# A hybrid mLSTM and DeltaNet block on one core: the turned tiles' transfers go from ScalarE to SyncE, a transpose is put off, and the bodies of four engines are ordered anew

## The chip, the cores and the metric

The kernel runs on one core of a Trainium2 chip. The metric is the device time of one execution in microseconds; the time of a kernel is the median of several executions. The profile shows one execution.

## The reference

The input x has 512 tokens of 2048 channels. The block computes, in float32:

```
u   = rmsnorm(x) * norm_w
p   = u @ w_in                          # 512 x 20528, split into the parts below
mLSTM branch:     q, k, v, o-gate, z-gate, i, f    # 8 heads, 128 wide q and k, 256 wide v
DeltaNet branch:  q, k, v, z-gate, beta, decay     # 16 heads of 128
merge gates:      g1, g2                           # 2048 each
h1 = rmsnorm_head(mlstm(q, k, v, i, f)) * w * sigmoid(o) * silu(z)
h2 = rmsnorm_head(deltanet(conv_silu(q), conv_silu(k), conv_silu(v), beta, decay)) * w * silu(z)
y  = x + sigmoid(g1) * (h1 @ w_out[0:2048]) + sigmoid(g2) * (h2 @ w_out[2048:4096])
out = rmsnorm(y) * final_norm_w
```

DeltaNet normalises q and k per token, and solves per chunk a unit lower triangular system, `(I + A) w = rhs` with `A[t, s] = beta[t] * (k[t] . k[s]) * decay[t, s]` for s < t.

## The kernel before, in words

**Weights and products.** Every product with a weight is made three times in a rounded format: both operands are split into a high and a low part, and hi x hi, hi x lo and lo x hi are added up. The weights come as 768 parts of 256 KB (640 of `w_in`, 128 of `w_out`). A part goes through three engines: SyncE issues its load into `wr` (L146, 4 buffers), ScalarE casts it to the high part `wh` (`split_hi`, L113), VectorE subtracts to get the low part `wl` (`split_lo`, L116; 4 buffers each), and TensorE makes 12 products of 512 columns with it (L212 to L214 in `proj_cm`, L242 to L244 in `proj_wide`, L939 to L941 at the output). Loads are written 4 parts ahead of their use, splits 3.

**Units.** The input projection runs in 12 units: an mLSTM unit of two heads and two DeltaNet units of two heads each, four times over (`m, d, d`, called a period below). A DeltaNet unit projects k, q, v and the z gate one after another (`dn_unit`). Behind each of the first three projections ScalarE copies the result out of PSUM into `yp` (L440), VectorE makes the convolution (L441, L443) and the SiLU (L447); behind the gate ScalarE makes a copy and a tanh `thz` (L452, L454).

**Turned tiles.** k, q, v and the normalised outputs are needed with tokens and channels exchanged. `turn` transposes 32 x 32 blocks on VectorE (L468), and the generator `travel` moves the blocks to their places through DRAM: four DMAs `td` of 64 KB (L476), and three ticks later one DMA back (L478). All five are issued by ScalarE.

**Side work.** While TensorE goes through the projections, generators are advanced by a tick after every 6 products; `start(gen, n)` starts one n ticks later and `yield n` puts its next piece n ticks off. `dn_front_k` starts KWAIT = 4 ticks after the k projection: products k k^T (L509), the matrix A goes through DRAM into `ls` (DMAs `ld` and `ls`), then the forward substitution of the 32 x 32 diagonal blocks, 31 steps of two VectorE instructions (`tmp` L548, `xi` L550), then the inverse goes through DRAM (`xd` L558, four DMAs, and `tt` L559), and VectorE turns it into `tn` (L560). `dn_front_q` makes the products of k and q (L568). `dn_back` starts 4 ticks after the gate projection: first the tokens' norms of the returned q (`token_norms`, ScalarE), then the products with `tn` (L601, L604) that build the full inverse. `dn_chain` then runs over the four chunks with the state (L653 to L691; L656 on VectorE between two products). `gated` multiplies by the gate TURN ticks after the last turn and writes to DRAM (`h_d`), from where the output stage reads.

**What sets the order.** TensorE's instructions run in the order in which they are written (`manual_schedule`). The order of the other engines' instructions is chosen by the framework's scheduler, by priority: `urgent(level)` and `high_priority` lift what stands in them (`PRIO = 1500` a level; loads and splits two levels), and an engine's instructions, DMA issues with them, run strictly in the order chosen. An instruction that waits holds all that stand behind it on its engine.

Of the kernel before, what the change touches and what calls it, by code (L numbers as in the profile page):

```python
# [17 lines left out]
NC = S // P  # L18
# [8 lines left out]
GNARROW = 4  # L27
GLAG = 3
KLAST = 4
TURN = 9  # L30
KWAIT, QWAIT = 4, 8
EPS = 1e-6
CAP = 15.0
# [6 lines left out]
BS = 32  # L40
# [5 lines left out]


@with_exitstack
def hybrid_block(
    ctx: ExitStack,  # L50
    tc: tile.TileContext,
    x: bass.AP,
# [13 lines left out]
    nc = tc.nc  # L66
# [102 lines left out]
    def urgent(level=1):  # L169
        return tc.high_priority(offset=level * PRIO)  # L170
# [4 lines left out]
    def start(gen, wait=0):  # L175
        active.append([gen, clock["t"] + wait])
# [251 lines left out]
    def row_bcast(r, name):  # L428
        t = wk.tile([P, NC, P], F32, tag="rb", name=name, bufs=3)
        nc.sync.dma_start(t.rearrange("p c t -> p (c t)"), rows_d[r, :].partition_broadcast(P))  # L430
        return t

    def bc(col, n):
        return col.unsqueeze(2).to_broadcast([P, NC, n])
# [29 lines left out]
    def turn(src, dst):  # L464


        o = dst if dst is not src else wk.tile([P, NC, P], F32, tag="to", name="to", bufs=2)
        V.transpose(o if len(src.shape) == 3 else o.rearrange("p n c -> p (n c)"), src)  # L468
        start(travel(o, dst), 1)

    def travel(o, dst):
        d = dr.tile([16, BS, 4, BS], F32, tag="td", name="td", bufs=8)
        ov = o.rearrange("p n (j c) -> p (n j) c", c=BS)
        with urgent(2):
            for a in range(4):
                nc.scalar.dma_start(d[:, :, a, :].rearrange("m r c -> r m c"), ov[a * BS:(a + 1) * BS])  # L476
        yield 3
        nc.scalar.dma_start(dst, d.rearrange("(n j) r a c -> (j r) n (a c)", n=NC))  # L478
        yield 1

    def gated(hn, w, g, kt):
        V.scalar_tensor_tensor(out=g, in0=hn.rearrange("p c t -> p (c t)"), scalar=w, in1=g, op0=ALU.mult,
                               op1=ALU.mult)
        nc.sync.dma_start(h_d[kt], g)
        yield 1

    def dn_front_k(hs, kq, u):
        for j in range(2):
            h = hs[j]
            rb = row_bcast(16 + h, "gb")  # L490
            dm = wk.tile([P, NC, P], F32, tag="dm", name="dm")
            G.affine_select(out=dm, in_=rb, pattern=[[0, NC], [1, P]], channel_multiplier=-1, base=0,
                            compare_op=ALU.is_ge, fill=-1e30)
            A.activation(rb, rb, AF.Exp)
            ge = wk.tile([P, NC], F32, tag="ge", name="ge", bufs=4)
            V.tensor_copy(ge, rb[:, :, P - 1])
            for c in range(NC):
                A.activation(dm[:, c, :], dm[:, c, :], AF.Exp, bias=ngam[:, c, h:h + 1])
            u["dm"].append((dm, rb, ge))
        nk = wk.tile([P, 2, NC], F32, tag="nk", name="nk")  # L500
        cs = wk.tile([P, 2, NC], F32, tag="cs", name="cs")

        for j in range(2):
            aq = wk.tile([P, NC, 2, P], F32, tag="aq", name="aq", bufs=4)
            u["aq"].append(aq)
            pk = psw.tile([P, NC, P], F32, tag="wk", name="pk")
            for c in range(NC):
                tsl = slice(c * P, (c + 1) * P)
                T.matmul(pk[:, c, :], kq[j][:, 0, tsl], kq[j][:, 0, tsl], start=True, stop=True)  # L509
            with urgent():  # L510
                V.tensor_tensor(out=aq[:, :, 0, :], in0=pk, in1=u["dm"][j][0], op=ALU.mult)
                jk = wk.tile([P, P], F32, tag="jd", name="jd", bufs=1)
                for c in range(NC):
                    V.scalar_tensor_tensor(out=jk, in0=aq[:, c, 0, :], scalar=1.0, in1=ident, op0=ALU.mult,
                                           op1=ALU.mult, accum_out=nk[:, j, c:c + 1])
            yield 1
        V.tensor_scalar(out=nk, in0=nk, scalar1=EPS, scalar2=None, op0=ALU.add)
        V.reciprocal(cs, nk)
        for j in range(2):
            V.tensor_tensor(out=cs[:, j, :], in0=cs[:, j, :], in1=beta[:, :, hs[j]], op=ALU.mult)  # L520
        u["nk"] = nk
        ld = dr.tile([2 * NC, 4, BS, BS], F32, tag="ld", name="ld", bufs=2)
        for j in range(2):
            aq = u["aq"][j]
            V.tensor_tensor(out=aq[:, :, 0, :], in0=aq[:, :, 0, :], in1=bc(cs[:, j, :], P), op=ALU.mult)
            for b in range(4):
                bs = slice(b * BS, (b + 1) * BS)
                nc.sync.dma_start(ld[j * NC:(j + 1) * NC, b, :, :].rearrange("c s t -> s c t"), aq[bs, :, 0, bs])

        for j in range(2):  # L530
            dm, eg, ge = u["dm"][j]
            G.tensor_tensor(out=dm, in0=dm, in1=bc(cs[:, j, :], P), op=ALU.mult)
        G.tensor_tensor(out=nk, in0=nk, in1=half, op=ALU.pow)


        ls = wk.tile([P, BS, BS], F32, tag="ls", name="ls", bufs=1)
        for q in range(4):
            nc.sync.dma_start(ls[q * NSYS:(q + 1) * NSYS], ld.rearrange("g b s t -> (g b) s t"))
        xi = wk.tile([P, BS // 4, BS], F32, tag="xi", name="xi", bufs=1)
        G.memset(xi, 0.0)  # L540
        for q in range(4):
            G.memset(xi.rearrange("p m t -> p (m t)")[q * NSYS:(q + 1) * NSYS, q:(BS // 4) * BS:BS + 4], 1.0)
        yield 4
        for i in range(BS - 1):
            n, m = BS - 1 - i, i // 4 + 1
            tmp = wk.tile([P, 80], F32, tag="tmp", name="tmp")
            tv = tmp[:, 0:n * m].rearrange("p (a b) -> p a b", b=n)
            V.tensor_tensor(out=tv, in0=ls[:, i, i + 1:BS].unsqueeze(1).to_broadcast([P, m, n]),  # L548
                            in1=xi[:, 0:m, i].unsqueeze(2).to_broadcast([P, m, n]), op=ALU.mult)
            V.tensor_tensor(out=xi[:, 0:m, i + 1:BS], in0=xi[:, 0:m, i + 1:BS], in1=tv, op=ALU.subtract)  # L550
            if i % 2:
                yield 1
        xd = dr.tile([2 * NC, 4, BS // 4, 4, BS], F32, tag="xd", name="xd", bufs=2)
        tt = wk.tile([P, 2 * NC, BS], F32, tag="tt", name="tt", bufs=1)
        tn = wk.tile([P, 2 * NC, BS], F32, tag="tn", name="tn", bufs=1)
        with urgent():
            for q in range(4):
                nc.sync.dma_start(xd[:, :, :, q, :].rearrange("g b m t -> (g b) m t"), xi[q * NSYS:(q + 1) * NSYS])  # L558
            nc.sync.dma_start(tt, xd.rearrange("g b m q t -> (b m q) g t"))  # L559
            V.transpose(tn.rearrange("p g m -> p (g m)"), tt.rearrange("p g t -> p (g t)"))  # L560
        u.update(tn=tn, tt=tt)

# [76 lines left out]
    def dn_chain(j, hs, kq, u):  # L639
# [50 lines left out]
        with urgent():  # L690
            V.tensor_tensor(out=os_, in0=po, in1=bc(rsd, P), op=ALU.mult)  # L691
        turn(os_, os_)
        start(gated(os_, normc[:, 32:33], u["g"][j], KT + h), TURN)

    def dn_unit(p):
# [5 lines left out]
        for j in range(2):  # L701
            conv_silu(ps[j], 16 + hs[j], kq[j][:, 0, :])
            ke = wk.tile([P, NC, P], F32, tag="ke", name="ke", bufs=4)
            turn(kq[j][:, 0, :], ke)
            u["ke"].append(ke)
        start(dn_front_k(hs, kq, u), KWAIT)
        ps = proj_cm(DN_Q + dcol)
        u["qn"] = []
        for j in range(2):
            conv_silu(ps[j], hs[j], kq[j][:, 1, :])  # L710
            qn = wp.tile([P, NC, P], F32, tag="tg", name="qn", bufs=3)
            turn(kq[j][:, 1, :], qn)
            u["qn"].append(qn)
# [84 lines left out]
    def ml_fin(j, hs, u):  # L798
        h = hs[j]
        hm = u["hm"][j]  # L800
        for i in range(2):
            hn = wk.tile([P, NC, P], F32, tag="os", name="mhn")
            turn(hm[i], hn)
            kt = 2 * h + i
            start(gated(hn, normc[:, 16 + kt:17 + kt], u["g"][j][i], kt), TURN)
            yield 1
# [168 lines left out]
        nc.sync.dma_start(out[c * P:(c + 1) * P, HD:D], hf[:, c, HD:D])  # L975


# [1 line left out]
_INS = ["x", "norm_w", "w_in", "ml_i_bias", "ml_f_bias", "ml_norm_w", "dn_conv_w",  # L979
        "dn_a_log", "dn_dt_bias", "dn_norm_w", "w_out", "final_norm_w"]  # L980
# [20 lines left out]
```

## Time and profile before

| | us |
|---|---|
| median of 3 runs | 2471.65 (2470.74 to 2472.73) |
| the profiled execution | 2470.49 |
| its span in the profile | 2468.9 |
| TensorE busy | 2328.0 (94%) |
| TensorE's weight loads busy | 1938.5 (79%) |
| VectorE busy | 1172.2 (47%) |
| ScalarE busy | 787.8 (32%) |
| GpSimd busy | 196.0 (8%) |
| mean granted TensorE clock | 0.974 |

PE is TensorE's matmul side, PEld its weight loads, DVE is VectorE, ACT ScalarE, POOL GpSimd, SP SyncE; ACTq and SPq are the engines' DMA issues. L116 is line 116 of the kernel before. `out<-in` names the tiles. In a row of waits stand the total in us, how often, and the longest. In a row of windows stand the stretch, its length, the busy time of PE, PEld, DVE, ACT and POOL with their instructions, the granted clock (1.00 is full), the DMA engines' share and GB/s. In a row of a timeline stand start and length, and in brackets how long the engine had been idle and what released it. In a row on a line's instructions stand the least, the median and the longest duration in ns.

### The profile page before, as it was taken

Reading aid. Unit: us, or ns where it says so; the run is one execution under the profiler, and the core shown is the slowest. Engines: PE = TensorE matmul, PEld = TensorE weight load, DVE = VectorE, ACT = ScalarE, POOL = GpSimd, SP = SyncE. Lnnn points to the kernel's source line nnn. Section 1 sums busy time; section 2 is a strip of 40 time slices with the busy share of each in tenths; the row PEclk is TensorE's granted clock in tenths of the full one; section 3 lists DMA queues with packets and bytes.
Section 4 is the critical chain, followed back from the end, with each engine's and each line's share of the span. In section 5 each row is a group of like instructions: output and inputs, shape, how many; then the busy total and the mean of one; then the engine's idle time right before and its main releaser. Section 6 shows DMA issues by size and latency. Waiting matters only on the chain.

```text
span 2468.9 us, 32143 instructions
## 1 busy us (share of the span) xinstructions
PE 2328.0 (94%) x11647; PEld 1938.5 (79%) x11647; DVE 1172.2 (47%) x2347; ACT 787.8 (32%) x1702; POOL 196.0 (8%) x261
## 2 busy tenths in 40 slices
PE   7999897999989799999879999988999999999998
PEld 5888776888877688887768888776998888888886
DVE  5533757433375744247574424757333322433434
ACT  5333242432324233232323323332333332322222
POOL 0000202000020200002020000202000000010110
PEclk9999998999999899999989999998999999999999
DMA  4433555453355545335554533554475453643433
GB/s 145 129 98 99 137 127 124 125 128 98 98 134 129 122 124 133 97 100 134 129 127 119 132 96 104 128 130 118 115 212 173 135 145 114 197 129 114 130 115 128
DMA packets 465440, 313.12 MB, mean 127 GB/s; under 512 B 234113, under 2 KB 404322, under 8 KB 465282
## 3 DMA queue, kind: packets, MB, share of 16 engines
q1 hardware_dynamic: 232898, 264.84, 37.3%
q10 hardware_dynamic: 232384, 46.23, 9.4%
q8 instruction: 91, 1.49, 0.2%
q14 instruction: 67, 0.55, 0.1%
HBM read 264.77 MB, written 46.20 MB: 126 GB/s over the span
## 4 chain that ended last, share of the span: by engine, by line
PE 80%; DVE 11%; DMA 3%; ACTq 2%; issue 2%; POOL 1%; ACT 1%; SPq 0%; DVEq 0%; POOLq 0%
PE pj L212 13%; PE pj L214 13%; PE pj L213 13%; PE py L940 5%; PE py L939 5%; PE py L941 5%; PE pg L244 4%; PE pg L242 4%; PE pg L243 4%; PE pv L244 2%; PE pv L243 2%; PE pv L242 2%; DVE tmp L548 2%; DVE xi L550 2%; ACTq L476 2%
## 5 line engine op out<-in xcount | busy, mean ns | idle before, releaser
L116 DVE TENSOR_TENSOR wl<-wr,wh 128x512 fp32r<-128x512 f32 x768 | 540.9, 713 | 929.2 <-ACT wh L113 909.9
L113 ACT CAST wh<-wr 128x512 fp32r<-128x512 f32 x768 | 470.8, 621 | 1406.3 <-PE pj L213 492.8
L212 PE MATMUL pj<-uh,wh 128*128 128x512 f32 x1792 | 740.0, 413 | 22.9 <-ACT thz L454 20.5
L214 PE MATMUL pj<-uh,wl 128*128 128x512 f32 x1792 | 711.6, 397 | 26.8 <-DVE wl L116 26.8
L213 PE MATMUL pj<-ul,wh 128*128 128x512 f32 x1792 | 709.3, 396 | 0.0
L214 PEld LDWEIGHTS pj<-uh,wl 128*128 128x128 f32 x1792 | 342.7, 191 | 106.9 <-DVE wl L116 32.3
L212 PEld LDWEIGHTS pj<-uh,wh 128*128 128x128 f32 x1792 | 345.1, 193 | 93.3 <-ACT thz L454 22.2
L213 PEld LDWEIGHTS pj<-ul,wh 128*128 128x128 f32 x1792 | 344.0, 192 | 65.1
L939 PE MATMUL py<-wh,hh 128*128 128x512 f32 x512 | 199.2, 389 | 0.0
L940 PE MATMUL py<-wl,hh 128*128 128x512 f32 x512 | 199.2, 389 | 0.0
L941 PE MATMUL py<-wh,hl 128*128 128x512 f32 x512 | 199.2, 389 | 0.0
L242 PE MATMUL pg<-wh,uh 128*128 128x512 f32 x384 | 149.4, 389 | 0.0
L243 PE MATMUL pg<-wl,uh 128*128 128x512 f32 x384 | 149.4, 389 | 0.0
L244 PE MATMUL pg<-wh,ul 128*128 128x512 f32 x384 | 149.4, 389 | 0.0
L939 PEld LDWEIGHTS py<-wh,hh 128*128 128x128 f32 x512 | 96.1, 188 | 20.1
L941 PEld LDWEIGHTS py<-wh,hl 128*128 128x128 f32 x512 | 96.1, 188 | 20.0
L940 PEld LDWEIGHTS py<-wl,hh 128*128 128x128 f32 x512 | 96.1, 188 | 19.8
L242 PE MATMUL pv<-wh,uh 128*128 128x512 f32 x256 | 99.6, 389 | 0.0
L243 PE MATMUL pv<-wl,uh 128*128 128x512 f32 x256 | 99.6, 389 | 0.0
L244 PE MATMUL pv<-wh,ul 128*128 128x512 f32 x256 | 99.6, 389 | 0.0
L243 PEld LDWEIGHTS pg<-wl,uh 128*128 128x128 f32 x384 | 72.1, 188 | 15.1
L244 PEld LDWEIGHTS pg<-wh,ul 128*128 128x128 f32 x384 | 72.1, 188 | 15.0
(243 smaller groups left out, 2339.0 us busy)
## 6 DMA issues: line engine op xcount, KB each, us to landing
wr<-in_w_in_dram SPq DMA_DIRECT2D x640, 256.0 KB, 2.8
wr<-in_w_out_dram SPq DMA_DIRECT2D x128, 256.0 KB, 3.0
td<-to ACTq DMA_DIRECT2D x128, 64.0 KB, 2.1
hr<-h_d SPq DMA_DIRECT2D x32, 256.0 KB, 3.4
tgl<-tg_d SPq DMA_DIRECT2D x32, 256.0 KB, 3.0
tg_d<-tgw SPq DMA_DIRECT2D x24, 256.0 KB, 3.7
xt<-in_x_dram SPq DMA_DIRECT2D x8, 512.0 KB, 8.2
gb<-rows_d SPq DMA_DIRECT2D x16, 256.0 KB, 3.6
```

What stands on the lines that cost most here:

```text
L113: A.copy(hi, src)
L116: V.tensor_tensor(out=lo, in0=src, in1=hi.bitcast(F32), op=ALU.subtract)
L212: T.matmul(ps[j], hi[:, k, wsl], uh[:, kt, :], start=(kt == 0), stop=False)
L213: T.matmul(ps[j], hi[:, k, wsl], ul[:, kt, :], start=False, stop=False)
L214: T.matmul(ps[j], lo[:, k, wsl], uh[:, kt, :], start=False, stop=(kt == KT - 1))
L242: T.matmul(ps[c], uh[:, kt, tsl], hi[:, 0, :], start=(kt == 0), stop=False)
L243: T.matmul(ps[c], uh[:, kt, tsl], lo[:, 0, :], start=False, stop=False)
L244: T.matmul(ps[c], ul[:, kt, tsl], hi[:, 0, :], start=False, stop=(kt == KT - 1))
L476: nc.scalar.dma_start(d[:, :, a, :].rearrange("m r c -> r m c"), ov[a * BS:(a + 1) * BS])
L939: T.matmul(ps[c], hh[base][:, kt, tsl], hi[:, 0, :], start=(kt == 0), stop=False)
L940: T.matmul(ps[c], hh[base][:, kt, tsl], lo[:, 0, :], start=False, stop=False)
L941: T.matmul(ps[c], hl[base][:, kt, tsl], hi[:, 0, :], start=False, stop=(kt == KT - 1))
```

## The change

- The five DMAs of a turned tile (L476, L478) are issued by SyncE and not by ScalarE. That is 352 `td` and 88 DMAs back. The DMA back becomes urgent, and stands four ticks behind the `td` and no longer three; `turn` starts `travel` two ticks later and no longer one.
- In `dn_front_k` the transpose of the inverse (L560) stands ten ticks behind its DMA and no longer directly behind it.
- TURN goes from 9 to 12.
- The body is put into a block whose order comes from the framework's timeline simulation. TensorE keeps the order written by hand, instruction for instruction. VectorE and GpSimd keep their number of instructions, SyncE goes from 1105 to 1545 and ScalarE from 1967 to 1527; the orders of all four differ.

```diff
-TURN = 9
+TURN = 12
...
-def hybrid_block(
+def hybrid_body(
...
-        start(travel(o, dst), 1)
+        start(travel(o, dst), 2)
 
     def travel(o, dst):
         d = dr.tile([16, BS, 4, BS], F32, tag="td", name="td", bufs=8)
         ov = o.rearrange("p n (j c) -> p (n j) c", c=BS)
         with urgent(2):
             for a in range(4):
-                nc.scalar.dma_start(d[:, :, a, :].rearrange("m r c -> r m c"), ov[a * BS:(a + 1) * BS])
-        yield 3
-        nc.scalar.dma_start(dst, d.rearrange("(n j) r a c -> (j r) n (a c)", n=NC))
+                nc.sync.dma_start(d[:, :, a, :].rearrange("m r c -> r m c"), ov[a * BS:(a + 1) * BS])
+        yield 4
+        with urgent(2):
+            nc.sync.dma_start(dst, d.rearrange("(n j) r a c -> (j r) n (a c)", n=NC))
         yield 1
...
             nc.sync.dma_start(tt, xd.rearrange("g b m q t -> (b m q) g t"))
+        yield 10
+        with urgent():
             V.transpose(tn.rearrange("p g m -> p (g m)"), tt.rearrange("p g t -> p (g t)"))
...
+def hybrid_block(tc, *args):
+    with tc.block(schedule_with_timeline_sim=True):
+        hybrid_body(tc, *args)
```

## What was predicted

> **What bounds the kernel now.** I read the page first, then TensorE's waits, then windows and timelines around each wait.
>
> ```profile
> span 2468.9 us, 32143 instructions
> PE 2328.0 (94%) x11647; PEld 1938.5 (79%) x11647; DVE 1172.2 (47%) x2347; ACT 787.8 (32%) x1702; POOL 196.0 (8%) x261
> PE 80%; DVE 11%; DMA 3%; ACTq 2%; issue 2%; POOL 1%; ACT 1%; SPq 0%; DVEq 0%; POOLq 0%
> PE pqk L568 <- DVE kq L447: 47.6, 4, 12.0
> PE pj L214 <- DVE wl L116: 26.8, 8, 6.8
> PE pj L212 <- ACT thz L454: 20.5, 4, 5.4
> PE pk L509 <- DVE kq L447: 14.5, 8, 2.0
> PE pj L212 <- ACT wh L113: 2.4, 4, 1.2
> 530.00:670.00 140.00, 140.00 (x627) 116.20 (x626) 45.41 (x70) 46.32 (x89) 3.77 (x4) 1.00 0.39 110
> ```
>
> TensorE (PE) is busy 94% of the span, and where nothing stops it (the window: us, then PE, PE weight load, DVE, ACT and POOL busy, granted clock, DMA share) it makes one matmul per 140/627 = 223 ns. The chain gives the other engines a fifth. The wait rows (total, times, longest) say where: 47.6 + 26.8 + 20.5 + 14.5 + 2.4 = 112 us. The counts 4 and 8 are one place in each of the four periods m, d, d (430 us each), or two. The waits cost a second time:
>
> ```profile
> 298.80:304.40 5.60, 5.60 (x13) 4.44 (x14) 1.75 (x3) 0.59 (x1) 0.74 (x5) 0.50 0.57 130
> 333.50:338.50 5.00, 5.00 (x12) 3.94 (x13) 3.48 (x6) 3.38 (x9) 0.00 (x0) 0.50 0.78 229
> 419.80:424.00 4.20, 4.20 (x14) 3.72 (x15) 3.99 (x11) 0.00 (x0) 1.96 (x2) 0.50 0.92 256
> 680.00:683.40 3.40, 3.40 (x12) 3.08 (x13) 1.86 (x6) 0.00 (x0) 0.00 (x0) 0.50 0.80 171
> 679.91 2.05 PE L509 MATMUL pk<-kq 128*128 128x128 f32 x8 [2.00 <-DVE kq L447]
> 250.61 1.16 PE L509 MATMUL pk<-kq 128*128 128x128 f32 x8 [2.00 <-DVE kq L447]
> ```
>
> Behind each long wait PE runs busy at a granted clock of 0.50: 5.6 + 5.0 + 4.2 + 3.4 = 18.2 us, half of it lost, 9 us a period, some 36 in all; I take 34, since the 3.4 us stand in some periods only. The short gaps are a matter of place: a 2.00-us gap before 679.91 left eight products at 2.05 us, an equal one before 250.61 at 1.16. A kernel with none of this would span 2468.9 - 112 - 34 = 2323 us.
>
> The causes are two queues.
>
> ```profile
> L548 DVE TENSOR_TENSOR tmp<-ls,xi 128x60 f32<-128x60 f32 (+24 forms) x31 | 8.6, 277 | 0.8
> L550 DVE TENSOR_TENSOR xi<-xi,tmp 128x60 f32<-128x60 f32 (+24 forms) x31 | 6.9, 223 | 0.9
> L116 DVE TENSOR_TENSOR wl<-wr,wh 128x512 fp32r<-128x512 f32 x5 | 3.4, 688 | 2.1 <-ACT wh L113 2.1
> 298.06 2.49 DVE L116 TENSOR_TENSOR wl<-wr,wh 128x512 fp32r<-128x512 f32 x4
> 419.69 2.08 PE L568 MATMUL pqk<-kq 128*128 128x128 f32 x8 [12.04 <-DVE kq L447]
> 326.49 4.72 ACTq L476 DMA_DIRECT2D td<-mhn  x8
> 331.25 0.62 ACT L113 CAST wh<-wr 128x512 fp32r<-128x512 f32 x1 [9.61 <-DMA td<-mhn]
> ACT wh L113 <- DMA td<-to: 92.9, 8, 17.5
> ACT wh L113 <- DMA td<-mhn: 69.9, 7, 10.7
> DVE tn L560 <- DMA tt<-xd: 51.8, 8, 7.1
> ```
>
> The first three rows are DVE's groups between 269.0 and 298.1 us: the 31 steps of the substitution (8.6 + 6.9 us) stand nearly in one piece, the low halves of the weights (L116) pile up and come four in a row at 298.06; PE starts at half rate at 298.8. At 419.69 the same run delays the q convolution, and PE waits 12.04 us for it. ACT stands 9.61 us behind its own issues of td before the cast at 331.25, with the gate's tanh (L454) behind it. And the turn of the inverse (L560) holds DVE 51.8/8 = 6.5 us each time, since it is queued right behind its DMA tt.
>
> **What the change removes.** The move of L476 and L478 to SyncE (SP) takes ACT's 163 us of waiting off it. The `yield 10` lets DVE go on while tt travels. The orders of DVE, ACT, POOL and SP are made anew; PE's, written by hand, is the same instruction for instruction, so waits can be placed. In the new DVE order a low half follows every few substitution steps, about every 12 products (2.7 us), and the casts stand ahead of other ACT work. Counting from the PE product on which the chain to a waiting product hangs, PE has 1.8 to 3.3 us of work where it had 0.1 to 4.6 (L509), over 7 where it had 1.4 to 6.0 (L568), over 7 for L116, 2.7 where it had 1.6 (L454). L509 stays close: conv and turn take about what its cover has, so I keep 0 to 1 us of it. The rest of the 112 and the 34 go: -146; what L509 keeps is counted below.
>
> **What it adds.** First the new late chain. The product L601 (dn_back) needs tn.
>
> ```profile
> 269.00:298.10 29.10, 23.75 (x112) 19.66 (x112) 26.56 (x85) 7.08 (x15) 3.89 (x4) 0.99 0.51 120
> L558 SPq DMA_DIRECT2D xd<-xi x32: 559/600/953, 298.2 to 1716.8; - x32
> xd<-xi SPq DMA_DIRECT2D x32, 32.0 KB, 2.1
> tt<-xd SPq DMA_DIRECT2D x8, 128.0 KB, 4.4
> L560 DVE STREAM_TRANSPOSE tn<-tt x8: 445/446/447, 306.8 to 1721.4; 128x256 f32<-128x256 f32 x8
> ```
>
> In the first DeltaNet unit of a period the last step of the substitution now stands behind splits, all the way from the q convolution's start, whose PE release is 240 matmuls ahead of L601: 240 x 0.223 = 53.5 us of cover. DVE's list in between: the old stretch took 29.1 us (window above), 9 more low halves at 0.69 add 6, the V convolutions and turns that now stand in it some 8: 43 us. Then four xd at 0.60 (2.4), xd's landing 2.1, tt's issue 0.4 and landing 4.4, tn 0.45: 9.8, and up to 4 for weight and h_d issues on SP ahead of them and for splits that wait for their own PE release. 43 + 10 to 14 = 53 to 57 of 53.5, and up to 5 more if steps in the list wait for ls. Bounds 0 to 10 us; I take 5, plus half rate behind it 2.8 (the 5.60 row, halved). What stands behind tn on DVE are low halves; `yield 10` puts other work ahead of it, so DVE itself should wait for tt for 0 to 3 us where it waited 6.5. In the second unit the same chain has about half a us to spare: 0 to 1.6, taken 0.
>
> Then the hops on one queue. SP takes over 352 td and 88 returns.
>
> ```profile
> L476 ACTq DMA_DIRECT2D td<-to x128: 309/514/1226, 315.3 to 1812.2; - x128
> L478 ACTq DMA_DIRECT2D qn<-td x16: 382/383/445, 300.9 to 1722.8; - x16
> L146 SPq DMA_DIRECT2D wr<-in_w_in_dram x640: 327/368/1390, 15.3 to 2088.6; - x160
> wr<-in_w_in_dram SPq DMA_DIRECT2D x640, 256.0 KB, 2.8
> td<-to ACTq DMA_DIRECT2D x128, 64.0 KB, 2.1
> ls<-ld SPq DMA_DIRECT2D x32, 128.0 KB, 3.3
> vt<-td ACTq DMA_DIRECT2D x16, 256.0 KB, 5.2
> SPq L146 <- DVE wl L116: 1403.6, 619, 14.2
> ```
>
> That is 352 x 0.514 + 88 x 0.383 = 215 us of issue, on a queue that now spends 1403.6 us waiting for a buffer; as a sum it is hidden. In bursts it isn't free: around the V projection 16 td, 4 returns and a landing of 2.1 to 2.6 stand in front of a weight load: 8.2 + 1.5 + 2.6 = 12.3 us. A load may be late by four parts (4 x 2.7) less its landing of 2.8 = 8 us before its split is late, and PE has the 7 us of L116 beyond: 15 > 12.3, so this price is 0. What pays are small chains. In the second unit the step L656, for which the state's product waits, stands on DVE behind a first substitution step that waits for ls: a landing of ld, taken as long as td's (2.1), an issue of 0.4 and the landing of ls (3.3) make 5.8 us, and PE has a little over 4 of work there: 1.6 late (0 to 2). The V copy L440, which frees the bank for PE, stands on ACT behind eight token norms that wait for the returned qn, so behind the burst of 12.3 us, which it has nearly covered: 1.5 (0 to 3). With L509's 0.5, 0.6 for the other places near zero, and 0.4 for a second half-rate stretch, a period has 5 + 2.8 + 1.6 + 1.5 + 0.5 + 0.6 + 0.4 = 12.4 us, four 50 us. Bounds: nothing at all, and 10 + 2.8 + 1.6 + 2 + 3 + 3 = 22 a period, 90 us.
>
> At the start:
>
> ```profile
> 18.52 3.03 PE L291 MATMUL put<-ident,xt 128*128 128x128 f32 x13 [2.00 <-DVE xt L284]
> 15.33 0.94 SPq L146 DMA_DIRECT2D wr<-in_w_in_dram  x2
> ```
>
> the last chunk's normalisation L284 now stands behind the first two low halves. Their weights are issued by 15.33 + 0.94 and land 2.8 later, at 19.1; a low half takes 0.7 and L284 about as much, so xt is ready near 20.5 and not at 18.5: the first product comes 2 us later (1 to 3). TURN = 12 only starts `gated` later; h_d is read in the output stage. Gate and output stages keep their order of work: 0.
>
> **Sum.** 2468.9 - 146 + 50 + 2 = 2375 span, 1.6 outside it (the profiled run took 2470.5), and 1.2 from there to the median of 2471.65: **2378 us**. With the bounds 0 and 90 for the added part the same sum gives 2328 to 2418.
>
> **The Trainium skill against two rows.** "DMA: Bandwidth & Descriptors", section "Issuing engines are not separate DMA queues", says that starting transfers from several engines only saves sequencer time, usually small beside the transfer. By that the move off ACT would be worth nothing and the rows L454 and L113 of PE's waits would stay: 2378 + 20.5 + 2.4 = 2401. The trace differs: a cast stood 9.61 us behind such issues. "TensorE: Matmul & The Clock Gate", Part 1, lets the clock fall after an idle window of about 3.4 us. By that the 2.00-us gap before 679.91 would cost no half rate, about 2 us less in each period that has it, and the sum would be some 4 us higher; the trace shows half rate there, so I don't follow it.
>
> **Rivals.** (A) Everything is covered, the late chain too, as its splits find their weights and nothing waits inside it. For it: in every other place the new order has more PE work over the chain than the old. Against: 53 to 57 us of list under 53.5 of cover. The added 50 us go: 2328. Chance 0.15.
>
> (B) Right in kind, but every hop is longer on one queue. For it: `vt<-td`, issued right behind a burst of td, lands after 5.2 us, where a weight load of the same 256 KB takes 2.8. If SP adds a third to the hops ahead of L601 (10 to 14 us become 14 to 18, so +4) and the second unit's chain comes 4 late as well with 2.5 of half rate, and the small chains double (+4 to 5), a period costs 12.4 + 15 = 27 us, four 110: 2438 (2425 to 2465). Against: SP sits idle for long stretches. Chance 0.17.
>
> (C) Slower: SP's bursts hold the weight loads. The price of a td on SP is not shown; the nearest rows are 0.31 to 1.23 us for the same transfer on ACT, and 0.56 to 0.95 for xd on SP. At 1.0 us, sixteen td, four returns and a landing take 16 + 1.5 + 2.6 = 20.1 us against 15 of reserve: 5.1 us of PE and 2.8 of half rate, in two bursts in each of eight units, 16 x 7.9 = 126 us on top of 2378: 2504. It decides from the point at which a burst costs 94/16 = 5.9 us, which is 0.87 us per td. For it: xd's 32 KB take 0.60 on SP, where td's 64 KB take 0.51 on ACT. Against: td's own median of 0.514. Chance 0.13.
>
> (D) The new order changes nothing that PE sees, as PE's own order stays: 2472. Every row of PE's waits names DVE or ACT, so this is thin: 0.02.
>
> **How the numbers follow.** The forecast has 0.53 (2340 to 2425) and is the likeliest. The range 2322 to 2455 takes in most of A, the forecast with the bounds of its terms, and three quarters of B: 0.12 + 0.53 + 0.13, about 0.8. The least that can be told from no change here is about 0.2%, 5 us. Faster are A, the forecast and B: 0.85; same is D: 0.02; slower is C: 0.13.
>
> **What would show it.** Right: the L568 and L454 waits of PE gone, L116 under 3 us, no cast of ACT behind td, a new PE wait on DVE tn at L601 or L604 of about 5 us, four times, granted clock near 0.99. Wrong: SP rows with td above 1 us, casts that wait for `wr`, or waits of over 10 us at L601 in all eight units.

## The result, and the profile after

The changed kernel takes 2400.11 us (median of 4, 2399.67 to 2401.08) where the kernel before took 2471.19 beside it: 0.9714 of the time, 95% interval 0.9697 to 0.973, 71 us less. The forecast was 2378, with 2322 to 2455: the direction and the places were right, the gain was 76% of the one forecast.

The page of the changed kernel, its rows for the span, the engines and the chain:

```profile
span 2398.5 us, 32163 instructions
PE 2311.6 (96%) x11647; PEld 1927.6 (80%) x11647; DVE 1144.5 (48%) x2347; ACT 800.1 (33%) x1702; POOL 192.6 (8%) x261
PE 80%; DMA 6%; DVE 6%; SPq 4%; issue 2%; ACT 1%; POOL 0%; DVEq 0%; POOLq 0%; ACTq 0%
```

The span is 70.4 us shorter: PE's busy time fell by 16.4 us, its idle time by 54. In the chain DVE has gone from 11% to 6%, ScalarE's DMA issues (ACTq) from 2% to 0%, and SPq and DMA stand there instead, with 10% between them. PE's waits in the changed kernel (total, times, longest; from L560 on, line numbers stand three higher than before):

```profile
PE p L604 <- DVE tn L563: 33.7, 7, 8.1
PE pnum L770 <- DVE c L780: 7.8, 4, 3.0
PE pj L212 <- ACT yp L440: 7.0, 7, 2.5
PE put L291 <- DVE xt L284: 5.6, 1, 5.6
PE pj L212 <- ACT thz L454: 3.1, 2, 1.7
PE pnum L770 <- DVE c L778: 1.7, 1, 1.7
PE pw L664 <- DVE r L659: 1.2, 2, 0.9
```

The old waits on kq, wl and wh are gone, all 91 us of them, and thz has 3.1 us left of 20.5. In their place stands mainly one that the kernel before did not have: the inverse tn for the first products of `dn_back`, 33.7 us in seven places. How it comes late is read from the timelines of SP and DVE (start, length, instruction) in the first DeltaNet unit:

```profile
320.33 2.86 SPq L476 DMA_DIRECT2D td<-mhn  x5
323.30 0.45 SPq L146 DMA_DIRECT2D wr<-in_w_in_dram  x1
323.85 0.42 SPq L479 DMA_DIRECT2D mhn<-td  x1
324.36 0.46 SPq L146 DMA_DIRECT2D wr<-in_w_in_dram  x1
324.99 0.36 SPq L479 DMA_DIRECT2D mhn<-td  x1
325.40 1.02 SPq L146 DMA_DIRECT2D wr<-in_w_in_dram  x2
326.47 2.94 SPq L559 DMA_DIRECT2D xd<-xi  x4
329.52 1.48 SPq L485 DMA_DIRECT2D h_d<-mg  x2
332.38 0.37 SPq L560 DMA_DIRECT2D tt<-xd  x1
319.60 0.17 DVE L551 TENSOR_TENSOR xi<-xi,tmp 128x8 f32<-128x8 f32 x1
335.28 0.45 DVE L563 STREAM_TRANSPOSE tn<-tt 128x256 f32<-128x256 f32 x1 [2.85 <-DMA tt<-xd]
335.88 1.06 PE L604 MATMUL p<-tn,aq 32*32 32x32 f32 x32 [8.13 <-DVE tn L563]
335.90:341.20 5.30, 5.30 (x42) 4.37 (x43) 0.40 (x1) 0.75 (x2) 2.23 (x5) 0.50 0.18 49
```

The last substitution step ends at 319.8. Its DMAs xd are first issued at 326.47, 6.7 us later, since SP first works through five td, two returns and four weight loads; tt follows at 332.38, behind xd's landing, and tn at 335.28. From the last step to a finished tn it is 16.0 us here, and 13.6 to 14.4 us in the first units of the other three periods. PE waits 8.13 us and then runs at a granted clock of 0.50 for another 5.3 (last row, a window).

### The profile page after: what moved, and what is told of

Its sections match the earlier page's. It is cut to its first block, busy times and chain, and to the rows that moved or that the text cites. A ratio compares the mean times of both kernels' runs of the same rounds, so it can differ in the third digit from the quotient of the medians.

```text
span 2398.5 us, 32163 instructions
## 1 busy us (share of the span) xinstructions
PE 2311.6 (96%) x11647; PEld 1927.6 (80%) x11647; DVE 1144.5 (48%) x2347; ACT 800.1 (33%) x1702; POOL 192.6 (8%) x261
## 4 chain that ended last, share of the span: by engine, by line
PE 80%; DMA 6%; DVE 6%; SPq 4%; issue 2%; ACT 1%; POOL 0%; DVEq 0%; POOLq 0%; ACTq 0%
PE pj L212 13%; PE pj L213 12%; PE pj L214 12%; PE py L944 5%; PE py L943 5%; PE py L942 5%; PE pg L242 4%; PE pg L243 4%; PE pg L244 4%; PE pv L243 2%; PE pv L244 2%; PE pv L242 2%; SPq L476 2%; PE pjt L227 1%; PE pjt L229 1%
## 5 line engine op out<-in xcount | busy, mean ns | idle before, releaser
L116 DVE TENSOR_TENSOR wl<-wr,wh 128x512 fp32r<-128x512 f32 x768 | 538.3, 703 | 849.8 <-ACT wh L113 835.5
L113 ACT CAST wh<-wr 128x512 fp32r<-128x512 f32 x768 | 475.8, 621 | 1237.8 <-PE pj L213 588.1
L242 PEld LDWEIGHTS pg<-wh,uh 128*128 128x128 f32 x384 | 72.1, 188 | 14.9
```

Of the source, the lines that this page charges most:

```text
L113: A.copy(hi, src)
L116: V.tensor_tensor(out=lo, in0=src, in1=hi.bitcast(F32), op=ALU.subtract)
L242: T.matmul(ps[c], uh[:, kt, tsl], hi[:, 0, :], start=(kt == 0), stop=False)
```

## The experiments

Each was timed beside the kernel before on the same chip; the ratios are to that time. The first question was which part of the change brings the gain. In both kernels the instructions of every engine stand in the same order whether the `yield 10` and the `with urgent()` under it are there or not, so that they change nothing. In the changed kernel travel's ticks and TURN do as little: with a return on SyncE that isn't urgent no instruction changes its place by them. What is left of the change is three parts: the block, the issuing engine, the urgency of the return.

**The block alone.**

```diff
+def hybrid_block(tc, *args):
+    with tc.block(schedule_with_timeline_sim=True):
+        hybrid_body(tc, *args)
```

> The kernel before, with its body in the timeline-simulation block and nothing else: td and the returns stay on ScalarE. Theory 1 (the gain comes from VectorE's order, in which low halves of the weights stand between the substitution steps): the PE waits on kq L447 (47.6 us) and wl L116 (26.8 us) go with the half rate behind them (20 us), and a wait on tn comes at the first products of dn_back, so 2385 to 2425 us. Theory 2 (the gain comes from taking the DMA issues off ScalarE): nothing of note, 2450 to 2475 us. If both are needed: about half of the gain, near 2435 us.

2386.84 us, 0.9663 (0.9647 to 0.9678): as theory 1 had it, and more than the whole gain. Five of PE's waits, and the three largest waits of ACT's casts for td:

```profile
PE pj L212 <- ACT wh L113: 10.8, 7, 2.5
PE pj L212 <- ACT thz L454: 9.8, 3, 4.7
PE p L601 <- DVE tn L560: 3.1, 3, 1.9
PE pk L509 <- DVE kq L447: 1.7, 4, 1.0
PE pj L214 <- DVE wl L116: 1.0, 2, 0.8
ACT wh L113 <- DMA td<-to: 79.8, 15, 11.5
ACT wh L113 <- DMA td<-mhn: 43.1, 9, 9.3
ACT wh L113 <- DMA td<-qn: 31.1, 3, 12.8
```

The waits on DVE (pqk 47.6, wl 26.8, pk 14.5) are gone without a transfer being moved. ACT still stands behind its td, 154 us of it, and PE waits 20.6 us for casts (wh) and thz. The expected wait on tn is hardly there: 3.1 us.

**The transfers without the block.** The kernel before with L476 and L478 on SyncE, the return urgent, travel's new ticks and TURN 12, no block.

```diff
-                nc.scalar.dma_start(d[:, :, a, :].rearrange("m r c -> r m c"), ov[a * BS:(a + 1) * BS])
-        yield 3
-        nc.scalar.dma_start(dst, d.rearrange("(n j) r a c -> (j r) n (a c)", n=NC))
+                nc.sync.dma_start(d[:, :, a, :].rearrange("m r c -> r m c"), ov[a * BS:(a + 1) * BS])
+        yield 4
+        with urgent(2):
+            nc.sync.dma_start(dst, d.rearrange("(n j) r a c -> (j r) n (a c)", n=NC))
```

> The kernel before, with the turned tiles' DMAs on SyncE, travel's ticks and urgency as in the change and TURN 12, but in the old scheduler. In this order the 62 substitution instructions stand in one piece on VectorE, with tn right behind them. Theory 1: ScalarE's waits for td go and PE's 20 us at thz with them, but the low halves wait for a run of about 15 us and a tn wait of 6 us, in all eight DeltaNet units, so no faster than before: 2470 to 2540 us, PE waits on wl L116 of 10 us and more. Theory 2: 2400 to 2440 us.

2647.53 us, 1.072 (1.0702 to 1.0738), slower by 178 us: far outside what either theory gave, and mostly by another wait than the one expected (wl L116 has 10.0 us in seven places, the longest 2.6):

```profile
PE p L602 <- DVE tn L561: 186.2, 8, 23.7
324.86 2.37 SPq L529 DMA_DIRECT2D ld<-aq  x5
328.87 1.82 SPq L539 DMA_DIRECT2D ls<-ld  x4
338.62 0.18 DVE L549 TENSOR_TENSOR tmp<-ls,xi 128x31 f32<-128x31 f32 x1
360.67 0.45 DVE L561 STREAM_TRANSPOSE tn<-tt 128x256 f32<-128x256 f32 x1 [6.53 <-DMA tt<-xd]
```

In this order SP issues the last five of the eight ld, and all ls, only at 325 to 331 us, where the kernel before issued ld and ls at 255 to 269 us; the substitution starts at 338.62 in one piece, and tn is about 23 us late in every DeltaNet unit. PE's waits at thz did not go either; they are 38.9 us. So the move with an urgent return costs 178 us in the old order, and 13 us in the block (2400.11 against 2386.84). How much of the 178 us is the move and how much the urgency is not shown: no run has the move alone without the block.

**The corners between.** The changed kernel with the five DMAs back on ScalarE, and the changed kernel with the old ticks and a return that isn't urgent:

```diff
-                nc.sync.dma_start(d[:, :, a, :]...      # first kernel: both DMAs on nc.scalar
+                nc.scalar.dma_start(d[:, :, a, :]...
```

> The changed kernel with the turned tiles' five DMAs back on ScalarE, all else as changed. Theory 1: 2390 to 2425 us, ScalarE casts behind td return as ScalarE's waits, PE pays for few of them. Theory 2: 2450 us and more.

```diff
-        yield 4                                         # second kernel; start(travel, 1), TURN = 9
-        with urgent(2):
-            nc.sync.dma_start(dst, ...
+        yield 3
+        nc.sync.dma_start(dst, ...
```

> The changed kernel with travel's old ticks: the turn starts it one tick later, the return comes three ticks behind the td and is not urgent, TURN 9; transfers on SyncE, timeline block. With ScalarE as issuer the new ticks cost 26 us (2412.6 against 2386.8). Theory 1a (the new ticks cost the same on SyncE): 2370 to 2380 us. Rival 1b (the ticks matter only on ScalarE, where casts stand behind the issues; on SyncE the late inverse decides, whose place in the queue is the same): 2393 to 2405 us.

The first kernel takes 2412.55 us, within theory 1. It has no PE wait on tn; PE waits 21.6 us for casts and 19.0 for thz instead, so PE pays more for them than expected. With the block on, the four corners are:

| | return as before | return urgent, new ticks and TURN |
|---|---|---|
| DMAs on ScalarE | 2386.84 (0.9663) | 2412.55 (0.9772, 0.9758 to 0.9787) |
| DMAs on SyncE | 2383.62 (0.9652, 0.9638 to 0.9667) | 2400.11 (0.9714) |

The block brings 82 us, the move to SyncE 3 or 12, and the urgency of the return takes 16 to 26 back. The 3 us are not clear of the noise: the intervals of the two ratios overlap. With ScalarE as issuer no run separates the urgency from the ticks, so the 26 us are of both. The second kernel came 4 us above what theory 1a gave. The rival (near 2400, as the late inverse decides) was right on the inverse, whose wait is as long in it (33.2 us), and wrong on the sum. How the urgency acts shows on SP and ACT near 410 us, first in the changed kernel, then in the one without urgency:

```profile
407.09 2.12 SPq L476 DMA_DIRECT2D td<-to  x4
409.31 1.02 SPq L479 DMA_DIRECT2D qn<-td  x2
410.38 1.05 SPq L479 DMA_DIRECT2D os<-td  x2
411.48 2.18 SPq L146 DMA_DIRECT2D wr<-in_w_in_dram  x4
412.54 0.31 ACT L462 ACTIVATE njk<-qn 128x128 f32<-128x128 f32 x1 [3.21 <-DMA qn<-td]
415.88 0.56 ACT L440 COPY yp<-pj 128x512 f32<-128x512 f32 x1
```

```profile
408.04 1.48 SPq L146 DMA_DIRECT2D wr<-in_w_in_dram  x3
410.08 0.50 SPq L478 DMA_DIRECT2D qn<-td  x1
411.57 0.58 ACT L440 COPY yp<-pj 128x512 f32<-128x512 f32 x1
```

The second kernel is 1.3 us ahead of the first there already (the last td are issued at 407.09 and 405.80). Beyond that, the urgent returns of qn and os stand in front of the weight loads, which come 2.1 us later, and eight token norms go in front of the copy yp on ACT, which comes 3.0 us later. Without urgency PE's waits on yp fall from 7.0 to 1.5 us in all, those on thz from 3.1 to none, and its busy time by 4.7 us: 13.3 us, about the 12.8 between the two spans (2398.5 and 2385.7; the profiled execution without urgency was the longest of its four, so the medians lie 16.5 apart). On SyncE the ticks and TURN have no part in this, since they don't touch the order there when the return isn't urgent.

**What the substitution costs, before and after.**

```diff
-        for i in range(BS - 1):
+        for i in range(1):
```

> The kernel before with one substitution step instead of 31 (the inverse is left unfinished): its price alone. Theory 1 (the run of steps on VectorE is what delays low halves and the q convolution): PE waits on kq L447 at L568 (47.6 us) and wl L116 (26.8 us) go with about 20 us of half rate, the 20 us at thz stay: 2365 to 2395 us. Rival (the run only happens to stand there, and the waits come from ScalarE's held queue): 2440 us and more.

> The changed kernel with one substitution step instead of 31. Theory 1 (the stretched substitution makes the inverse late): the PE wait on tn at L604 (33.7 us) goes with about 10 us of half rate, 2345 to 2362 us, and it is below the kernel before without the steps by the 20 us at thz and their half rate. Rival (the hops on SyncE alone make it late): the wait stays, 2385 us and more.

Before: 2396.33 us, 0.9702 (0.9687 to 0.9716), just above the 2395 expected; wl is gone, but pqk keeps 11.1 of 47.6 us and pk all of its 14.5 (14.6 here), so these come from what else stands on DVE. After: 2373.25 us, 0.9608 (0.9592 to 0.9624), above the 2362 expected: the wait on tn is gone whole, but pnum (10.4 + 1.5 us) and yp (9.6) grew. So the substitution cost 74 us before (2470.11 beside it) and 27 after, and the kernels without it still differ by 23 us. The new order does not free DVE of work; it takes about two thirds of this price away from PE.

**The late inverse.** Two edits, one on either end of its chain: dn_back later, and xd and tt first on SP.

```diff
-        start(dn_back(hs, kq, u), 4)
+        start(dn_back(hs, kq, u), 8)
```

> The changed kernel with dn_back started 8 ticks behind the gate projection instead of 4 (24 products, about 5.4 us more for the inverse to arrive). Theory 1 with the late inverse as the largest loss left: the PE wait on tn at L604 (33.7 us in seven places) falls to under 10 us, half rate behind it goes, 2355 to 2375 us. Rival (the wait moves to the next product of the chain, or to the state products of the mLSTM unit that follow): 2393 to 2405 us.

```diff
-        with urgent():
+        with urgent(4):
             for q in range(4):
                 nc.sync.dma_start(xd[:, :, :, q, :]...
```

> The changed kernel with the inverse's DMAs (xd and tt) raised above the weight loads, so that in the first unit of a period xd stands ahead of two weight loads, two returns and two more loads on SyncE, and tt ahead of h_d and a load. Theory 2 (SyncE's queue makes the inverse late: in the trace xd is issued 6.6 us behind the last substitution step): the wait at L604 falls by 3 to 6 us in each first unit, from 6.3 to 8.1 us to 1 to 4 us, 2370 to 2388 us. Rival (the list on VectorE decides and xd is early enough): 2397 to 2403 us.

2371.73 us (0.9608, 0.9593 to 0.9622) and 2379.0 us (0.9628, 0.9613 to 0.9642). Both are where the theories had them. In the first the wait at L604 falls from 33.7 to 5.8 us; part of it moves, as PE's wait for yp grows from 7.0 to 13.2. In the second the wait falls to 16.7 us, by what SP gains:

```profile
322.97 2.63 SPq L559 DMA_DIRECT2D xd<-xi  x4
327.04 0.36 SPq L560 DMA_DIRECT2D tt<-xd  x1
PE p L604 <- DVE tn L563: 16.7, 5, 4.2
```

xd is issued 3.5 us earlier, tt 5.3, and PE's wait there is 3.7 us where it was 8.1. The list on DVE is the same up to the last step; SP's queue is what made the difference. In this unit tn no longer waits for tt, but stands behind DVE instructions of which the first (L483) waits 5.38 us for a returned mhn.

**Together.** dn_back at 8 ticks, the return not urgent, xd and tt first (called e9 below):

> The changed kernel with three edits together: dn_back 8 ticks behind the gate projection, the return not urgent (with the old ticks and TURN 9, which leave the order of every engine's instructions as it is), xd and tt raised above the loads. Alone they gave 28, 16 and 21 us; the first and the third act on the same wait at L604. Theory (different waits, so the first two add up and the third takes what is left of tn's wait, 5.8 us and its half rate): 2400 - 28 - 16 - 6 = 2350 us, 2343 to 2358. Rival (they all work on the same slack, the next chain is close behind): 2364 to 2373 us.

2348.26 us, 0.951 (0.9494 to 0.9526): as the sum said, and the fastest here beside the next. PE has no wait on tn any more. Three of the waits left:

```profile
PE pj L214 <- DVE wl L116: 6.4, 4, 2.3
PE pnum L769 <- DVE c L779: 5.8, 4, 2.3
PE pj L212 <- ACT yp L440: 2.2, 4, 0.7
```

Two priorities more (norms not urgent, c raised by two levels; called e10, with the changed kernel's ticks and TURN):

```diff
-            with urgent():
-                A.activation(jk, pk[:, c, :], AF.Square, accum_out=dst[:, c:c + 1])
+            A.activation(jk, pk[:, c, :], AF.Square, accum_out=dst[:, c:c + 1])
...
-                with urgent():
+                with urgent(3):
                     if c1 is None:
```

> As e9, and two priorities more: the tokens' norms in dn_back are not urgent, so the copy yp L440 need not stand behind them on ScalarE, and the mLSTM state c (L778, L780), for which PE waited 6 to 10 us in all, is raised. If these chains are what is left: 6 to 12 us below e9. Rival (they move by a place or two and PE sees nothing): within 3 us of e9.

2349.12 us (0.9507, 0.9493 to 0.9521): the rival, no difference. And the same with the DMAs on ScalarE (called e11, with the ticks of the kernel before):

> The kernel before with the timeline block and the same edits (dn_back at 8 ticks, xd and tt raised, norms not urgent, c raised), the turned tiles' DMAs on ScalarE: what the issuing engine is worth once the late inverse is out of the way. Theory (casts and thz stand behind the issues on ScalarE, 20 us of PE's waits in the block-only kernel): 10 to 25 us above e10. Rival (the issuer is worth no more than the 3 us found with the old ticks): within 5 us of e10.

2371.46 us (0.9598, 0.9584 to 0.9612), 22 us above e10, within the theory's range. PE waits 15.6 us for yp and 9.8 for thz, as against 2.3 and none; for casts, which the theory named, it waits only 1.0. The issuing engine is worth 22 us once the inverse is out of the way. In the change as made it was worth 12, since with SyncE PE waited 33.7 us for tn, and with ScalarE not at all.

## Why the prediction was right, and where its size was off

**Removed: right.** All of the waits on kq and wl and 17.4 of thz's 20.5 us are gone, 109 of the 112 counted. The reason was right in the main: low halves between the substitution steps. The block alone takes these waits away, and without the steps wl's wait and 36.5 of pqk's 47.6 us are gone. The steps don't explain the 14.5 us at pk, which stay without them and go with the new order; which part of that order frees them is not shown. Two of the reasons given were not right. The `yield 10` moves no instruction: that DVE waits for tt only 2.9 us each time (23.3 in eight), as forecast, comes from the block's order, so there the number was right by luck. And the move to SyncE isn't what most of the gain hangs on. In the block it takes away the 20.6 us of PE's waits for casts and thz, as forecast, but with the returns as before it brings a wait of 33.2 us on tn (3.1 with the block alone) and 9.3 on pnum (0.7), so that it gains next to nothing.

**The late inverse at L604: right place, price too low.** Forecast 5 us in each first unit, bounds 0 to 10, and 0 in the second: the four first units waited 8.1, 6.8, 6.6 and 6.3, the second 2.8, 1.0 and 2.1, 33.7 in all against 20. Three terms of the sum were too small, as the four first units show:

- The tail (four xd, two landings and tn) was to take 9.8 us with up to 4 more. It took 16.0, 13.8, 14.4 and 13.6 us. SP's queue held xd for 6.7, 5.2, 5.4 and 5.2 us of that, and xd landed after 4.0 us and not 2.1 (medians); tt was quicker (2.9 us and not 4.4).
- DVE's list, from the start of the q convolution to the last substitution step, was to take 43 us. It took 52.0, 55.3, 51.5 and 53.3 (from 267.73 to 319.77 in the first). In it DVE waits 3.2 to 5.6 us for ls and 1.6 to 3.8 for a returned mhn; the forecast named up to 5 us for ls beside the 43, and nothing for mhn.
- The cover, 240 matmuls of PE, was to last 53.5 us. It lasted 60 to 63: PE itself waits in it for pnum (1.0 to 3.8 us) and runs part of it at half rate (granted clock 0.96 to 0.97 over these stretches). What remains of the excess is not taken apart here.

List and cover were each some 7 to 12 us too short and nearly cancel. That the forecast came within 1.3 to 3.1 us of each first wait is therefore in part luck. The start of the list in the first unit, the landings, and td's issue on SP (for rival C below):

```profile
267.73 0.47 DVE L441 TENSOR_SCALAR kq<-yp,convc 128x512 f32<-128x512 f32 x1
xd<-xi SPq DMA_DIRECT2D x32, 32.0 KB, 4.0
tt<-xd SPq DMA_DIRECT2D x8, 128.0 KB, 2.9
L476 SPq DMA_DIRECT2D td<-to x128: 303/496/806, 309.7 to 1742.0; - x128
```

**The small chains.** yp: 1.5 a period forecast, 7.0 in all measured; the place looked at, near 415 us, has the reason given (behind the eight norms that wait for qn). L509's rest, 0.5 a period forecast: none. L656, now L659: 1.6 a period forecast, 1.2 in all. The start: +2 us forecast, +3.6 measured. Missing from the forecast: pnum, 9.5 us in all, where PE waits for the mLSTM state c from DVE, and 3.1 left at thz. Forecast waits added: 4 x 9.2 + 2 = 39 us; measured 33.7 + 9.5 + 7.0 + 3.6 + 3.1 + 1.2 = 58.

**Half rate.** Forecast 34 us gone, 13 added, so 21 off PE's busy time; measured 16.4 off it. The two shortfalls, 19 and 5 us, are about the 23.5 between the forecast span of 2375 and the measured 2398.5.

**The rivals.** (C) needed td at 0.87 us on SyncE; they take 0.496 there (row above). But in the old order the move with an urgent return did come out slower, mostly by the late inverse (186.2 us of PE's waits; 36.8 for casts). (D) is refuted by the changed kernel and by the block alone, where PE's order is the same. (A) did not come, as the late chain has its price; with three more edits e9 comes to 2348, still 20 us above it. Of (B) the longer landing of xd came true, and a late second unit in small (1.0 to 2.8 us in three of the four).

**Two rules of the Trainium skill.** What "DMA: Bandwidth & Descriptors" of the Trainium skill says in "Issuing engines are not separate DMA queues", that several issuers save only sequencer time, fits in kind: what left ScalarE's queue are issues of about 0.5 us per td. What they hold up behind them was not small here: 22 us between e10 and e11. "TensorE: Matmul & The Clock Gate" of the Trainium skill, Part 1, has the clock fall after an idle window of about 3.4 us; here half rate came behind shorter waits once more (last section), and the measurement decides.

## What to carry to other kernels

When an engine order is made anew, ask of each chain that crosses engines where its last hop stands in a DMA queue: here four small DMAs stood 5 to 7 us in SP's queue, and raising them and the one behind them gained 21 us, more than the 3 to 12 that moving 440 issues brought. Raise the short DMAs at the end of a chain above the prefetches and not the returns nobody is waiting for yet, and move a consumer that is fixed in TensorE's order by a few ticks before tuning its producers. Test the parts of a bundle by themselves: of this one, the block gave 82 us, the move 3 to 12, the urgent returns took 16 to 26, and the rest moved no instruction on SyncE. A part's worth also hangs on the order around it: the move with urgent returns cost 178 us without the block and 13 with it.

## What the hardware showed that was not expected

TensorE's granted clock fell behind waits of under 3 us, and not always at once. Behind a wait of 1.59 us and, two products later, one of 0.37, it ran for 3 us at half rate (first window below, of the changed kernel, granted clock 0.54), though neither gap alone is as long as the 2.00-us one of the kernel before that left the rate full. It looks as if the two gaps add up, but that is not shown: behind a single wait of 2.80 us TensorE first ran 1.4 us at the full rate (granted clock 1.00 from 445.5 to 446.9), and only then at half (second window, 0.50). So the half rate at 300 us can also be the late answer to the first gap alone.

```profile
298.93 0.70 PE L770 MATMUL pnum<-c,mkq 128*128 128x257 f32 x2 [1.59 <-DVE c L780]
300.00 0.60 PE L212 MATMUL pj<-uh,wh 128*128 128x512 f32 x1 [0.37 <-ACT yp L440]
300.00:303.00 3.00, 3.00 (x8) 2.32 (x9) 2.93 (x10) 2.75 (x8) 0.00 (x0) 0.54 0.31 86
445.47 0.69 PE L604 MATMUL p<-tn,aq 32*32 32x32 f32 x32 [2.80 <-DVE tn L563]
447.20:449.80 2.60, 2.60 (x8) 2.01 (x7) 0.40 (x1) 0.00 (x0) 1.44 (x3) 0.50 0.56 125
```
